# Seven products per feature added up in PSUM by two accumulating banks, and for two more features in each feed-forward block

## The chip, the cores and the metric

The kernel runs on one core of a Trainium2 chip. The metric is the device time of one execution in microseconds (us); three runs of the kernel before took 2045.32 to 2047.19 us, median 2046.94.

The engines are named as in the profile: PE is TensorE (matmuls; PEld are its weight loads), DVE is VectorE, ACT is ScalarE, POOL is GpSimd, SP is SyncE, which issues the transfers.

## The reference

Two layers of a decoder over 512 tokens of 1024 features in float32. Each layer is a feed-forward block, a mixer (gated linear attention in the first layer, retention in the second) and a second feed-forward block, each with a residual and a layer norm. The change is in the four feed-forward blocks:

```
def swiglu(x, w_in, w_out):                       # x [512, 1024], D_FF = 2816
    gate, up = jnp.split(x @ w_in, 2, axis=-1)    # w_in [1024, 5632]
    return (jax.nn.silu(gate) * up) @ w_out       # w_out [2816, 1024]

h = layer_norm(DN_ALPHA * h + 0.5 * swiglu(h, ...), g, b)
```

## The kernel before, in words

**Precision.** Every float32 operand is split exactly into hi + lo, two parts of a type that PE multiplies at full pace; a product takes three matmuls (hi hi, lo hi, hi lo), written by `mm3` (L151 to L153). ACT casts the hi part (L105 for weights, L369 for sums of h), DVE subtracts for the lo part (L106, L370).

**Weights.** They stream in granules of 1 MiB in the order of use. `Stream.prepare` splits a granule into slots of 128 x 1024: five of them, and two of 128 x 512. `Stream.next` hands out a granule and prepares the next. A plain granule takes two slots. A granule for seven products takes three and a small one, since two sums of blocks of its weights are formed (L129 to L131) and split as well.

**A feed-forward block.** The 2816 hidden features are 22 features of 128 each ("feature" below means such a group). The plain form (`feature_major`) gives gate and up of one feature with 48 matmuls of 512 columns. The form of seven products (`seven_products`; Strassen's method after Winograd over halves of the tokens, of the 1024 inputs, and of gate and up) takes 7 x 12 = 84 matmuls of 256 columns. Its products read either quarters of h as they are (`hThi`, `hTlo`) or four sums of such quarters, S0 to S3 (`Shi`, `Slo`), which `operand_sums` forms once per block, after features 0 and 1 in the program: for each of two halves c the raw sums (L364, L374, L377, L379, L382), each split by L369 and L370. The raw sums live in buffers of the tags "gate" and "up", two of each; `activate` takes its own tile `sg` from the tag "gate" as well. Features 0 to 3 of a block are plain, 4 to 21 go through seven products. After a feature ACT takes silu, DVE multiplies by up (L394), and the result is split into `ahi` (L397) and `alo` (L398), the operands of the output product. The granules of the output product ("out" in the plan, tiles `po`) lie between later features.

**PSUM.** There are six banks of the pool `acc` and two of `tr`. One feature of the seven-products form takes two of each. DVE and ACT add the products up: ACT copies the first one (L343, L349), DVE does five additions (L346 to L355).

**Order.** The order of the instructions on each engine is fixed ahead of time by a planner. It takes what is ready by its own estimate of the times, what comes first in the program going first; buffers of a tag are given out in the order of the program. On the chip each engine goes through its list in that order, with semaphores between engines.

Of the kernel before, what the change touches and what calls it, by code (L numbers as in the profile page):

```python
# [17 lines left out]
P = 128  # L18
# [8 lines left out]
FAST = frozenset(f for f in range(4, NF))  # L27
# [11 lines left out]
def _ffn_plan():  # L39
    """The order of a feed-forward block's granules: ("in", f) for gate and up of  # L40
    128 features, ("out", c, i) for four units of the output product of chunk c,
    which lie between the features of the next chunk."""
    plan = []
    for c, (f0, f1) in enumerate(CHUNKS):
        n = 0
        for f in range(f0, f1):
            plan.append(("in", f))
            if c and (f - f0) % 2 == 0 and n < (CHUNKS[c - 1][1] - CHUNKS[c - 1][0]) // 2:
                plan.append(("out", c - 1, n))
                n += 1  # L50
    return plan + [("out", len(CHUNKS) - 1, i) for i in range((CHUNKS[-1][1] - CHUNKS[-1][0]) // 2)]


def _fast():
    """The granules of feed-forward weights that seven products take."""
    r, at = set(), 0
    plan = _ffn_plan()
    for mixer in (0, GH * 3 + GH, 0, RH * 6 + 2 * RH):
        at += mixer
        r |= {at + i for i, x in enumerate(plan) if x[0] == "in" and x[1] in FAST}  # L60
        at += len(plan)
    return r
# [3 lines left out]
def tile_decoder(ctx: ExitStack, tc: tile.TileContext, a: dict, out: bass.AP):  # L66
# [9 lines left out]
    # ---------------------------------------------------------------- weights  # L76
    class Stream:
        """The weights, 1 MiB at a time in the order of their use, each split
        exactly into two float32r parts."""
# [21 lines left out]
        def parts(self, slot, src, at=0):  # L101
            """src as hi + lo."""
            n = src.shape[-1]
            hi, lo = (x[:, at:at + n] for x in slot)
            nc.scalar.copy(hi, src)  # L105
            nc.vector.tensor_sub(lo, src, hi.bitcast(F32))  # L106

        def prepare(self, i):
            if i >= self.n or i in self.split:
                return  # L110
            self.load(i)
            w = self.loaded[i]
            blk = lambda slot, c: tuple(x[:, c * B:(c + 1) * B] for x in slot)  # noqa: E731
            if i not in fast:
                s = [self.place.pop((i, c))() if (i, c) in self.place else self.slot() for c in range(2)]
                for c in range(2):
                    if i:
                        self.parts(s[c], w[:, 2 * c * B:2 * (c + 1) * B])
                    else:
                        for at in ((0, B), (B, 0))[c]:  # L120
                            self.parts(s[c], w[:, 2 * c * B + at:2 * c * B + at + B], at)
                self.split[i] = [blk(x, c) for x in s for c in range(2)]
                return
            b11, b12, b22, b21 = (w[:, c * B:(c + 1) * B] for c in range(4))
            s11, sb, st, su = (self.slot(n) for n in (1, 2, 2, 2))
            self.parts(s11, b11)
            self.parts(sb, w[:, 2 * B:])
            t13, t24 = (self.sums_pool.tile([P, 2 * B], F32, tag="sums", name="sums", bufs=2) for _ in range(2))
            nc.vector.tensor_sub(t13, w[:, B:3 * B], w[:, :2 * B])  # L129
            nc.vector.tensor_sub(t24[:, :B], b22, t13[:, :B])  # L130
            nc.vector.tensor_sub(t24[:, B:], b21, t24[:, :B])  # L131
            self.parts(st, t24)
            self.parts(su, t13)
            self.split[i] = {"b11": blk(s11, 0), "b22": blk(sb, 0), "b21": blk(sb, 1), "t2": blk(st, 0),
                             "t4": blk(st, 1), "t1": blk(su, 0), "t3": blk(su, 1)}
# [12 lines left out]
    def mm3(ps, l, r, start, stop):  # L148
        """One K tile of a float32 product: (hi + lo) x (hi + lo), with the three
        passes that reach float32's precision."""  # L150
        nc.tensor.matmul(ps, l[0], r[0], start=start, stop=False)  # L151
        nc.tensor.matmul(ps, l[0], r[1], start=False, stop=False)  # L152
        nc.tensor.matmul(ps, l[1], r[0], start=False, stop=stop)  # L153
# [4 lines left out]
    # ---------------------------------------------------------------- start  # L158
# [38 lines left out]
    # ---------------------------------------------------------------- layer norm  # L197
# [8 lines left out]
    def rsqrt(tp, out_, in_, eps, n, scale=1.0):  # L206
        """(scale * (in_ + eps)) ** -0.5"""
# [4 lines left out]
    def layer_norm(tp, t, gb, last):  # L212
        """h[t] <- LN(h[t]); its transpose into hT."""
# [22 lines left out]
    # ---------------------------------------------------------------- products  # L236
    def feature_major(w, ranges, ps=None):
        """out[feature, token] of 2 tiles of 128 features."""
# [14 lines left out]
    def two_granules_ahead():  # L253
        """The first two granules after a layer norm: the first half of the tokens
        is taken first, while the norm of the second half ends."""
# [7 lines left out]
    def token_major(t, ws2, ps):  # L263
        """out[token, 512 columns] of one token tile."""
        for k in range(KD):
            mm3(ps, pick(hT[0], slice(None), k, slice(t * P, (t + 1) * P)), ws2[k // 4][k % 4], k == 0, k == KD - 1)
# [3 lines left out]
    def add_out(t, half, ps, first, tp=None):  # L270
        """h[t] <- alpha * h[t] + ps, or h[t] + ps; with tp, what the layer norm
        needs of it."""
# [10 lines left out]
    class Units:  # L283
        """Units [P, 512] of the coming granules, four in each."""
# [9 lines left out]
    def out_steps(lhs, n, first, halves=(0, 1), tp=None):  # L294
        """h[:, half] += lhs^T @ W for all tokens, one K tile after the other: the
        steps, each to be given its unit."""
# [14 lines left out]
    def out_by_tokens(lhs, n, units, halves, first, tail=None, tp=None):  # L311
        """The same, one token tile after the other."""
# [9 lines left out]
    # ---------------------------------------------------------------- feed-forward  # L322
    def seven_products(w, s, tp):
        """gate and up [feature, token] of 128 features with the seven products of
        Winograd's form of Strassen's method, over halves of the tokens, of the
        features of h and of the outputs (gate and up)."""
# [3 lines left out]
        def bank(pool, tag):  # L330
            return pool.tile([P, 2, H], F32, tag=tag, name="products")

        def product(ps, a_, b_):
            b_ = tuple(x.rearrange("p (k c) -> p k c", k=4) for x in w[b_])
            for k in range(4):
                mm3(ps, pick(b_, slice(None), k), pick(a_, slice(None), k), k == 0, k == 3)
            return ps

        gate, up, u, v = (tp.tile([P, 2, H], F32, tag=n, name=n, bufs=1 + (n in "gateup")) for n in ("gate", "up", "u", "v"))
        x, y, z, q = (bank(*b) for b in ((pacc, "acc"), (pacc, "acc"), (ptr, "tr"), (ptr, "tr")))  # L340
        # v = (p1, p1 + p6 + p7), u = (p1 + p6, p1 + p6 + p7)
        p1 = product(x[:, 0], a11, "b11")
        nc.scalar.copy(v[:, 0], p1)  # L343
        product(z[:, 0], a12, "b21")
        p6 = product(x[:, 1], s[1], "t2")
        nc.vector.tensor_add(u[:, 0], v[:, 0], p6)  # L346
        p7 = product(y[:, 0], s[2], "t3")
        nc.vector.tensor_add(u[:, 1], u[:, 0], p7)
        nc.scalar.copy(v[:, 1], u[:, 1])  # L349
        product(z[:, 1], a22, "t4")  # L350
        nc.vector.tensor_add(gate, v, z)
        p5 = product(y[:, 1], s[0], "t1")
        nc.vector.tensor_add(up, u, p5[:, None, :].broadcast_to([P, 2, H]))
        p3 = product(q[:, 0], s[3], "b22")
        nc.vector.tensor_add(up[:, 0], up[:, 0], p3)  # L355
        return [x.rearrange("p a b -> p (a b)") for x in (gate, up)]

    def operand_sums(tp):
        """The sums of blocks of h that seven_products takes, split."""
# [26 lines left out]
    def ffn(layer, which, ln, last=False, first=False):  # L386
        with tc.tile_pool(name=f"ffn{layer}{which}", bufs=2) as tp:
# [3 lines left out]
            def activate(f, gate, up):  # L391
                sg = tp.tile([P, T], F32, tag="gate", name="sg")
                nc.scalar.activation(sg, gate, AF.Silu)
# [46 lines left out]
    # ---------------------------------------------------------------- mixers  # L440
    def gated_transpose(tp, y, n, gcol, bufs=1):
        """yT[n tiles of 128 features][tokens] * g, split."""
# [13 lines left out]
    def gla(ln):  # L456
        with tc.tile_pool(name="gla", bufs=1) as tp:
# [22 lines left out]
            def gates(pg):  # L480
                """la[head] <- log sigmoid of the gates, [key feature, token]."""
# [19 lines left out]
            def decays(hd):  # L501
                """exp of the gates' sums: within chunks of 64, and within blocks of 128
                from their start and to their end."""
# [15 lines left out]
            def qk_of(ps, d):  # L519
# [4 lines left out]
                v4 = lambda x: x.rearrange("p (n two c) -> p n two c", two=2, c=CH)  # noqa: E731  # L524
# [9 lines left out]
            def vr_of(g, between):  # L534
                """The values, and 2 silu(r); `between` is called before the last tokens."""
# [209 lines left out]
def _weights(i):  # L745
    """All matrices as granules [P, G] in the order in which the kernel takes them."""
    def blocks(w):
        """[D, 256] as four blocks of [4 x 128, 128]: (0, 0), (0, 1), (1, 1), (1, 0)."""
# [47 lines left out]
def _constants():  # L796
    """Tables that depend on the shapes alone."""
# [35 lines left out]
```

## Time and profile before

| | |
|---|---|
| median of 3 runs | 2046.94 us (2045.32 to 2047.19) |
| span of the profiled execution | 2044.7 us; the page gives no time of its own for what lies around the span |
| PE busy | 2031.3 us, 99% |
| DVE busy | 1516.3 us, 74% |
| ACT busy | 796.8 us, 39% |
| matmuls | 12364 |
| moved from and to HBM | 205.00 MB, mean 100 GB/s |
| granted TensorE clock, mean | 0.998 |

[...] Matmuls overlap in PE's pipeline, so the duration of one (0.28 us for 256 columns) is longer than the distance between the starts of two; paces are read from starts, or from counts in a window. A releaser in brackets behind a row ("<-PE fm") is what ended the engine's idle time before it.

### The profile page before, as it was taken

Reading aid. Unit: us, or ns where it says so; the run is one execution under the profiler, and the core shown is the slowest. Engines: PE = TensorE matmul, PEld = TensorE weight load, DVE = VectorE, ACT = ScalarE, POOL = GpSimd, SP = SyncE. Lnnn points to the kernel's source line nnn. Section 1 sums busy time; section 2 is a strip of 40 time slices with the busy share of each in tenths; the row PEclk is TensorE's granted clock in tenths of the full one; section 3 lists DMA queues with packets and bytes.
Section 4 is the critical chain, followed back from the end, with each engine's and each line's share of the span. In section 5 each row is a group of like instructions: output and inputs, shape, how many; then the busy total and the mean of one; then the engine's idle time right before and its main releaser. Section 6 shows DMA issues by size and latency. Waiting matters only on the chain.

```text
span 2044.7 us, 29592 instructions
## 1 busy us (share of the span) xinstructions
PE 2031.3 (99%) x12364; PEld 1808.6 (88%) x12364; DVE 1516.3 (74%) x2152; ACT 796.8 (39%) x1131; POOL 37.2 (2%) x56
## 2 busy tenths in 40 slices
PE   8999999999999999999999999999999999999998
PEld 7999998888889999998999998888888889999997
DVE  7888888745588888887888888554545468888886
ACT  5443433632234344343434443333232324443441
POOL 0000000000000000000000000000000000000000
PEclk9999999999999999999999999999999999999999
DMA  6322223112222222341322223222222222322322
GB/s 213 118 104 104 104 96 132 65 65 80 103 83 104 104 103 104 104 145 42 124 103 104 104 86 142 104 69 93 78 88 78 88 75 104 117 91 102 109 99 83
DMA packets 33637, 205.00 MB, mean 100 GB/s; under 512 B 5056, under 2 KB 5184, under 8 KB 10592
## 3 DMA queue, kind: packets, MB, share of 16 engines
q1 hardware_dynamic: 33504, 203.12, 28.2%
q8 instruction: 97, 1.59, 0.3%
q14 instruction: 36, 0.29, 0.0%
HBM read 201.00 MB, written 2.10 MB: 99 GB/s over the span
## 4 chain that ended last, share of the span: by engine, by line
PE 99%; DVE 0%; DMA 0%; ACT 0%; issue 0%; DVEq 0%
PE products L151 12%; PE products L152 12%; PE products L153 12%; PE po L151 10%; PE po L152 10%; PE po L153 10%; PE fm L152 5%; PE fm L151 5%; PE fm L153 5%; PE pvr L151 2%; PE pvr L152 1%; PE pvr L153 1%; PE pgg L151 1%; PE pgg L152 1%; PE pv L153 1%; PE pgg L153 1%
## 5 line engine op out<-in xcount | busy, mean ns | idle before, releaser
L106 DVE TENSOR_TENSOR wlo<-wf,whi 128x512 fp32r<-128x512 f32 (+1 forms) x362 | 399.6, 1108 | 97.6 <-ACT whi L105 97.2
L105 ACT CAST whi<-wf 128x512 fp32r<-128x512 f32 (+1 forms) x362 | 345.8, 958 | 300.6 <-PE po L153 130.6
L151 PE MATMUL products<-Shi,whi 128*128 128x256 f32 x1152 | 325.7, 283 | 0.0
L153 PE MATMUL products<-Shi,wlo 128*128 128x256 f32 x1152 | 325.6, 283 | 0.0
L152 PE MATMUL products<-Slo,whi 128*128 128x256 f32 x1152 | 325.6, 283 | 0.0
L151 PE MATMUL po<-whi,ahi 128*128 128x512 f32 x704 | 274.8, 391 | 0.0
L152 PE MATMUL po<-wlo,ahi 128*128 128x512 f32 x704 | 274.4, 390 | 0.0
L153 PE MATMUL po<-whi,alo 128*128 128x512 f32 x704 | 274.0, 389 | 0.0
L152 PE MATMUL products<-hTlo,whi 128*128 128x256 f32 x864 | 243.0, 281 | 0.0
L151 PE MATMUL products<-hThi,whi 128*128 128x256 f32 x864 | 242.9, 281 | 0.0
L153 PE MATMUL products<-hThi,wlo 128*128 128x256 f32 x864 | 242.0, 280 | 0.0
L153 PEld LDWEIGHTS products<-Shi,wlo 128*128 128x128 f32 x1152 | 220.4, 191 | 0.0
L151 PEld LDWEIGHTS products<-Shi,whi 128*128 128x128 f32 x1152 | 220.0, 191 | 0.3
L152 PEld LDWEIGHTS products<-Slo,whi 128*128 128x128 f32 x1152 | 220.2, 191 | 0.0
L105 ACT CAST whi<-sums 128x1024 fp32r<-128x1024 f32 x144 | 150.3, 1047 | 159.8 <-DVE h L277 87.7
L151 PE MATMUL fm<-hThi,whi 128*128 128x512 f32 (+1 forms) x592 | 202.9, 343 | 5.2 <-ACT hThi L183 5.2
L152 PE MATMUL fm<-hTlo,whi 128*128 128x512 f32 (+1 forms) x592 | 203.0, 343 | 0.0
L153 PE MATMUL fm<-hThi,wlo 128*128 128x512 f32 (+1 forms) x592 | 202.5, 342 | 0.0
L106 DVE TENSOR_TENSOR wlo<-sums,whi 128x1024 fp32r<-128x1024 f32 x144 | 175.7, 1222 | 24.0 <-ACT whi L105 24.0
L152 PEld LDWEIGHTS products<-hTlo,whi 128*128 128x128 f32 x864 | 163.0, 189 | 1.4
L151 PEld LDWEIGHTS products<-hThi,whi 128*128 128x128 f32 x864 | 162.9, 189 | 1.4
L153 PEld LDWEIGHTS products<-hThi,wlo 128*128 128x128 f32 x864 | 163.5, 189 | 0.0
(185 smaller groups left out, 3431.0 us busy)
## 6 DMA issues: line engine op xcount, KB each, us to landing
wf<-in_wts SPq DMA_DIRECT2D x179, 1024.0 KB, 4.8
ln_b<-in_ln_b SPq DMA_DIRECT2D x6, 512.0 KB, 3.7
ln_g<-in_ln_g SPq DMA_DIRECT2D x6, 512.0 KB, 5.2
xs<-in_xT SPq DMA_DIRECT2D x8, 256.0 KB, 5.3
h<-in_x SPq DMA_DIRECT2D x4, 512.0 KB, 7.8
out_h<-h SPq DMA_DIRECT2D x8, 256.0 KB, 2.0
wf<-in_wts SPq DMA_DIRECT2D x4, 256.0 KB, 5.8
dm<-in_decay SPq DMA_DIRECT2D x4, 256.0 KB, 3.2
```

Source lines behind the costliest of these rows:

```text
L105: nc.scalar.copy(hi, src)
L106: nc.vector.tensor_sub(lo, src, hi.bitcast(F32))
L151: nc.tensor.matmul(ps, l[0], r[0], start=start, stop=False)
L152: nc.tensor.matmul(ps, l[0], r[1], start=False, stop=False)
L153: nc.tensor.matmul(ps, l[1], r[0], start=False, stop=stop)
```

## The change

Features 2 and 3 of each block go through seven products too (`FAST` begins at 2). Inside `seven_products`, four products are added into one PSUM bank x one after the other, two into a bank z, and one goes to a bank y. After each step but the last the running sum is copied out of the bank by ACT into a tile `part` before the next product adds to it; DVE's five additions become three of 256 columns. The second half of gate is left in x, and `activate` reads it from there. The bank tiles are half as large, but each still takes a bank (two of `acc`, one of `tr` per feature). `operand_sums`, the plan, the numbers of slots and the tags "gate" and "up" stay. A parameter lowers the scratch for DMAs that are generated on the fly.

```diff
-FAST = frozenset(f for f in range(4, NF))
+FAST = frozenset(f for f in range(2, NF))
...
-    def mm3(ps, l, r, start, stop):
+    def mm3(ps, l, r, start, stop, more=False):
...
+        nc.tensor.matmul(ps, l[0], r[0], start=start, stop=False, skip_group_check=more)
...
         def bank(pool, tag):
-            return pool.tile([P, 2, H], F32, tag=tag, name="products")
+            return pool.tile([P, H], F32, tag=tag, name="products")
...
+        def product(ps, a_, b_, start=True):
...
+                mm3(ps, pick(b_, slice(None), k), pick(a_, slice(None), k), start and k == 0, k == 3, not start)
+
+        def kept(ps, n):
+            nc.scalar.copy(part[:, n], ps)
+            return part[:, n]
+
+        part = tp.tile([P, 4, H], F32, tag="part", name="part", bufs=2)
+        gate, up = (tp.tile([P, 2, H], F32, tag=n, name=n) for n in ("gate", "up"))
+        x, y, z = (bank(*b) for b in ((pacc, "acc"), (ptr, "tr"), (pacc, "acc")))
+
+        product(x, a11, "b11")
+        p1 = kept(x, 0)
+        product(y, a12, "b21")
+        nc.vector.tensor_add(gate[:, 0], p1, y)
+        product(x, s[1], "t2", False)
+        p16 = kept(x, 1)
+        product(z, s[0], "t1")
+        p5 = kept(z, 3)
+        product(x, s[2], "t3", False)
+        p167 = kept(x, 2)
+        product(z, s[3], "b22", False)
+        nc.vector.tensor_add(up[:, 1], p167, p5)
+        nc.vector.tensor_add(up[:, 0], p16, z)
+        product(x, a22, "t4", False)
+        return gate, up, x
...
-            def activate(f, gate, up):
+            def activate(f, gate, up, late=None):
                 sg = tp.tile([P, T], F32, tag="gate", name="sg")
-                nc.scalar.activation(sg, gate, AF.Silu)
+                if late is None:
+                    nc.scalar.activation(sg, gate, AF.Silu)
+                else:
+                    nc.scalar.activation(sg[:, :H], gate[:, 0], AF.Silu)
+                    nc.scalar.activation(sg[:, H:], late, AF.Silu)
+                    up = up.rearrange("p a b -> p (a b)")
...
-    nc = bacc.Bacc("TRN2", target_bir_lowering=False, num_devices=1)
+    nc = bacc.Bacc("TRN2", target_bir_lowering=False, num_devices=1, dynamic_dma_scratch_size=1024)
```

## Rows read from the trace of the kernel before

**Rows 1.** The page's parts 1 and 4: engines' busy time, shares of the chain.

```profile
PE 2031.3 (99%) x12364; PEld 1808.6 (88%) x12364; DVE 1516.3 (74%) x2152; ACT 796.8 (39%) x1131; POOL 37.2 (2%) x56
...
PE 99%; DVE 0%; DMA 0%; ACT 0%; issue 0%; DVEq 0%
```

**Rows 2.** Waits of PE: who for whom, us in total, times, longest.

```profile
PE fm L151 <- ACT hThi L183: 5.2, 1, 5.2
PE po L151 <- ACT yhi L450: 0.3, 1, 0.3
```

**Rows 3.** Windows: stretch, length, busy us per engine, granted clock, DMA.

```profile
core 0: us, PE busy (x) PEld busy (x) DVE busy (x) ACT busy (x) POOL busy (x), PEclk, DMA share, GB/s
602.11:624.51 22.40, 22.40 (x98) 18.05 (x97) 21.89 (x32) 11.41 (x18) 0.00 (x0) 1.00 0.27 93
645.42:665.43 20.01, 20.01 (x169) 20.00 (x168) 15.55 (x22) 10.16 (x15) 0.00 (x0) 1.00 0.22 80
376.00:379.40 3.40, 3.40 (x8) 2.71 (x9) 2.07 (x3) 3.38 (x8) 0.00 (x0) 0.51 0.40 169
```

**Rows 4.** Timeline of DVE, second block: start, duration, engine, line, operation, tiles, shapes.

```profile
589.66 1.30 DVE L364 TENSOR_TENSOR hsum<-hThi,hTlo 128x512 f32<-128x512 f32 x2
596.70 0.69 DVE L394 SCALAR_TENSOR_TENSOR sg<-sg,fm 128x512 f32<-128x512 f32 x1 [5.74 <-PE fm L153]
...
600.18 0.69 DVE L364 TENSOR_TENSOR hsum<-hThi,hTlo 128x512 f32<-128x512 f32 x1
...
604.86 0.69 DVE L398 TENSOR_TENSOR alo<-sg,ahi 128x512 fp32r<-128x512 f32 x1
...
606.59 0.68 DVE L364 TENSOR_TENSOR hsum<-hThi,hTlo 128x512 f32<-128x512 f32 x1
607.19 1.22 DVE L106 TENSOR_TENSOR wlo<-wf,whi 128x1024 fp32r<-128x1024 f32 x1
608.33 0.68 DVE L377 TENSOR_TENSOR hsum<-hsum 128x512 f32<-128x512 f32 x1
608.93 0.69 DVE L130 TENSOR_TENSOR sums<-wf,sums 128x512 f32<-128x512 f32 x1
...
618.57 0.69 DVE L370 TENSOR_TENSOR Slo<-hsum,Shi 128x512 fp32r<-128x512 f32 x1
```

**Rows 5.** Timelines of PE and DVE: starts of feature 2, ends of S1.

```profile
30.31 0.40 PE L151 MATMUL fm<-hThi,whi 128*128 128x512 f32 x1
602.11 0.40 PE L151 MATMUL fm<-hThi,whi 128*128 128x512 f32 x1
951.71 0.40 PE L151 MATMUL fm<-hThi,whi 128*128 128x512 f32 x1
...
46.20 0.69 DVE L370 TENSOR_TENSOR Slo<-hsum,Shi 128x512 fp32r<-128x512 f32 x1
968.17 0.69 DVE L370 TENSOR_TENSOR Slo<-hsum,Shi 128x512 fp32r<-128x512 f32 x1
```

**Rows 6.** Timeline of PE in the first block's feature 4.

```profile
55.54 0.40 PE L151 MATMUL products<-Shi,whi 128*128 128x256 f32 x2
```

**Rows 7.** Timeline of PE ahead of the slow stretch.

```profile
372.29 3.69 PE L487 MATMUL pz<-gl,wgate 32*128 32x512 f32 x8
```

**Rows 8.** Timelines of PE and ACT at the end of a product.

```profile
652.32 0.28 PE L152 MATMUL products<-hTlo,whi 128*128 128x256 f32 x1
...
652.69 1.05 ACT L105 CAST whi<-sums 128x1024 fp32r<-128x1024 f32 x1 [0.49 <-PE products L152]
653.65 0.62 ACT L393 ACTIVATE sg<-gate 128x512 f32<-128x512 f32 x1
```

**Rows 9.** Groups by line: busy us, mean ns, idle before and releaser.

```profile
L129 DVE TENSOR_TENSOR sums<-wf 128x1024 f32<-128x1024 f32 x72 | 87.9, 1221 | 1.0
L351 DVE TENSOR_TENSOR gate<-v,products 128x512 f32<-128x512 f32 x72 | 49.5, 688 | 70.4 <-PE products L153 68.5 <-ACT v L349 1.9
L343 ACT COPY v<-products 128x256 f32<-128x256 f32 x72 | 26.9, 373 | 37.3 <-PE products L153 37.0
```

More of the change, by code (lines that the diff above doesn't have):

```diff
@@ L146, in tile_decoder @@
     ws = Stream()
-    def mm3(ps, l, r, start, stop):
-        nc.tensor.matmul(ps, l[0], r[0], start=start, stop=False)
-        nc.tensor.matmul(ps, l[0], r[1], start=False, stop=False)
-        nc.tensor.matmul(ps, l[1], r[0], start=False, stop=stop)
+    def mm3(ps, l, r, start, stop, more=False):
+        nc.tensor.matmul(ps, l[0], r[0], start=start, stop=False, skip_group_check=more)
+        nc.tensor.matmul(ps, l[0], r[1], start=False, stop=False, skip_group_check=more)
+        nc.tensor.matmul(ps, l[1], r[0], start=False, stop=stop, skip_group_check=more)
     def pick(pair, *idx):
@@ L330, in bank @@
         def bank(pool, tag):
-            return pool.tile([P, 2, H], F32, tag=tag, name="products")
-        def product(ps, a_, b_):
+            return pool.tile([P, H], F32, tag=tag, name="products")
+        def product(ps, a_, b_, start=True):
             b_ = tuple(x.rearrange("p (k c) -> p k c", k=4) for x in w[b_])
             for k in range(4):
-                mm3(ps, pick(b_, slice(None), k), pick(a_, slice(None), k), k == 0, k == 3)
-            return ps
-        gate, up, u, v = (tp.tile([P, 2, H], F32, tag=n, name=n, bufs=1 + (n in "gateup")) for n in ("gate", "up", "u", "v"))
@@ L340, in seven_products @@
[L340 to L356, printed above, removed]
+                mm3(ps, pick(b_, slice(None), k), pick(a_, slice(None), k), start and k == 0, k == 3, not start)
+        def kept(ps, n):
+            nc.scalar.copy(part[:, n], ps)
+            return part[:, n]
```

## The prediction

> **What bounds the kernel now.** Read the page's first and fourth parts before anything else [rows 1]: TensorE (PE) is busy for 99% of the span and the chain of work that ended last is 99% PE. Then the list of waits, for PE alone [rows 2]: two waits in the whole run, 5.2 us at the start and 0.3 us. So the time is the number of matmuls times their pace, and any wait that the change puts on PE is paid in full. The table of windows gives the paces [rows 3]. From 602.11 to 624.51 PE does features 2 and 3 of the second feed-forward block in the plain form, 96 matmuls of 512 columns (2 x 48; the count includes those on the edges): 22.40/96 = 0.2333 us. From 645.42 to 665.43 it does two features with seven products, 168 matmuls of 256 columns: 20.01/168 = 0.1191 us. The same rows carry the warning: VectorE (DVE) is busy for 21.89 of the 22.40 us under features 2 and 3, against 15.55 of 20.01 later. Something is being made ready there.
>
> The timeline of DVE over that place says what [rows 4]: the sums of blocks of h (L364 to L382, their splits at L370) that every seven-products feature needs. Feature 2 starts at 602.11; the split of S1's second half, needed by a feature's third product, starts at 618.57 and ends 0.69 later, at 619.26, 17.1 us after the start of feature 2. In the first block it ends at 46.20 + 0.69, 16.6 us after feature 2's start at 30.31; in the third at 968.17 + 0.69, 17.1 us after 951.71 [rows 5]. Before the change nothing minds: features 2 and 3 are plain, and cover 22.4 us.
>
> **The change, part by part.** I sum on the profiled execution: 2044.7 us of span, and the 2.2 us by which the median of the runs shown (2046.94) exceeds it I take as lying around the span and unchanged.
>
> (a) Two more features in each of four blocks go through seven products. Removed: 48 x 0.2333 = 11.20 us each; added: 84 x 0.1191 = 10.00. Eight times 1.20: **-9.6 us**. That is the whole gain, since PE does the same seven products per feature otherwise.
>
> (b) The sums lose their cover. Call feature 2's start t. Its first two products read h itself and take 24 x 0.119 = 2.86 us; the third reads S1, so S1's second half is wanted at t + 2.86 + 0.71 = t + 3.6. It cannot be there: the chain stands in a queue for buffers. The raw sums share two buffers of tag "gate" with the two activations before them. In the trace, after two sums of the other tag (589.66), DVE does nothing for 5.74 us before 596.70 although h is complete; the first "gate" sum runs at 600.18, and the second at 606.59, behind alo of feature 1 at 604.86 [rows 4]. The edit leaves tags, counts and order alone. From the second "gate" sum to the end of S1's second half it is 619.26 - 606.59 = 12.67 us, of which L106 at 607.19 (1.14 to the next start) and L130 at 608.93 (0.60) are foreign; without them 10.9. Lower bound: alo's 0.60 from 604.86, then 10.9: 616.4 or t + 14.3. Upper bound: features 2 and 3 now want the seven-products split of their weights too. On DVE one such split is 1.14 for L129 (1.22 busy [rows 9], but a 1024-wide row lets the next start after 1.14, as at 607.19), twice 0.60, 0.60 for b11 and 3 x 1.14 = 6.4 us, against 2 x 1.14 = 2.3 plain; the 4.1 more for feature 2, if none of it falls into the idle stretch, puts it at t + 21.2. I take the row itself, t + 17.1: the extra split fits the idle 5.74 us, and the foreign work inside the chain is only exchanged.
>
> What can PE do in those 17.1 us? Feature 2's first two products (2.86), the first halves of its third and of the one on S0 (1.42, their sums come first), the two products of feature 3 that read h (2.86), and one of feature 4 (1.43): 8.6. The order on each engine is a planner's by readiness, not the program's: at 55.54, in the first block, two L151 matmuls on S start one behind the other [rows 6], where the program writes each L151 with its L152 and L153 behind it: one of the two was drawn forward from a later product. So PE idles about 8.5 us in each block, with 5.0 at the lower bound (t + 14.3, and 9.3 filled by half a product more) and 17.6 at the upper one (t + 21.2, and nothing filled but 3.6). Four blocks: **+34 us**, bounds +20 and +70.
>
> (c) The clock. After 372.29, where PE had eight small matmuls in 3.69 us [rows 7], the granted clock is 0.51 for 3.4 us (376.00 to 379.40 [rows 3]): 1.7 us lost. PE's idle stretch here is at least as empty. One such loss in each block: **+6.8 us**, none to two per block as bounds (0 to +13.6).
>
> (d) The accumulating banks. The second product into a bank waits until ScalarE has copied the first; a product into another bank lies between (1.43 us). A copy costs 0.37 [rows 9], so alone it is hidden. But three products on, the last split of the next weights becomes free to start: in [rows 8] such a cast starts at 652.69, 0.37 us after the start of the last-but-one matmul of the product that frees its buffer (652.32), and ScalarE's next instruction starts 0.96 later. The new copy of p1+p6+p7 would stand behind that cast: it would end 0.37 + 0.96 + 0.37 = 1.70 after that matmul, and the accumulating product is due 0.24 + 1.43 = 1.67 after it. Late by 0.03, and with an exposed answer and weight load perhaps 0.25 for each of 80 features: 0 to +20. I take the 0.03: **+2 us**.
>
> [...]
>
> (e) At nothing: fewer DVE additions (three of 256 columns and two of 512, each of the latter 0.69 [rows 9], become three of 256) and more ScalarE copies (two become four, and silu is halved) work on engines with room in the steady stretch, DVE 15.55 and ScalarE 10.16 busy in 20.01 us [rows 3]; PE's cover there is the 10 us of each feature. They would cost only through (d). The single banks, the smaller scratch of the DMA and the dropped comments issue nothing.
>
> Sum: -9.6 + 34 + 6.8 + 2 = +33; 2044.7 + 2.2 + 33 = **2080 us**.
>
> **The rivals.**
>
> *Faster: the sums arrive in time.* If the raw sums ran in DVE's idle 5.74 us, or enough foreign products filled PE, only (a) would remain: 2046.9 - 9.6 = 2037. For it: DVE is free there. Against it: the decisive second "gate" sum comes behind alo of feature 1, which itself starts 2.75 us after t (604.86 against 602.11), and the edit moves neither. It decides from S1 ready at t + 3.6. Chance 0.09. If the idle time is just eaten by the gain, 2.4 us per block, the time stays within 0.2% (4 us, about what a measurement of this kernel tells from no change): 2047, chance 0.06.
>
> *Slower still: nothing fills the wait.* PE then idles 17.1 - 3.6 = 13.5 us a block, with two clock losses: -9.6 + 54 + 13.6 + 2 = +60, 2107 us. For it: a blocked matmul blocks those behind it if the order was planned on other times than the chip's. Against it: [rows 6]. Chance 0.14. [...]
>
> *Slower by the copies.* If every feature pays 0.25 us in (d), 18 us come on top: 2098. For it: the cast becomes ready one matmul before the copy. Against it: the planner can put a matmul of the next feature into so short a gap. Chance 0.10.
>
> **How the numbers follow.** The forecast has 0.55, in a range of its own of 2057 (the lower bound of (b), no clock loss, no late copies) to 2105; 0.06 more I leave to slower mixtures of these. Slower by over 0.2%: 0.55 + 0.14 + 0.10 + 0.06 = 0.85; within 0.06; faster 0.09. The range takes in the forecast, the late copies and half of the unfilled case: 2050 to 2112.
>
> **What would show it.** In PE's waits, four long ones on DVE's Slo at products of features 2, near 33, 605 and 955 us and in the fourth block, 5 to 14 us each block; a granted clock of half after them; PE's products at 0.119 us elsewhere. The split of S1's second half still 14 to 21 us after the start of feature 2. For (d), many short waits of products on a ScalarE copy, once a feature. The prediction is wrong if PE's list of waits stays as short as before, if S1 is ready within 4 us of feature 2's start, or if PE's waits in the blocks sum to less than 10 us.

## The result, and the profile after

The changed kernel takes 2083.38 us (median of 4 runs, 2082.48 to 2084.57), the kernel before 2046.81 us beside it: a ratio of 1.0178, 95% interval 1.0164 to 1.0193. It is slower by 36.6 us, 37 in round figures. The profiled execution has a span of 2082.6 us, against 2044.7 before.

From the page of after, its parts 1 and 4, against [rows 1]:

```profile
PE 2048.1 (98%) x12652; PEld 1831.4 (88%) x12652; DVE 1459.4 (70%) x2072; ACT 875.9 (42%) x1403; POOL 37.2 (2%) x56
...
PE 96%; DVE 3%; ACT 0%; issue 0%; DMA 0%; DVEq 0%; SPq 0%; ACTq 0%
```

DVE is in the chain now, with 3% of the span. The list of PE's waits in after (who for whom, us in total, times, longest), against [rows 2], says where:

```profile
PE products L151 <- ACT Shi L374: 14.0, 8, 2.7
PE fm L151 <- ACT hThi L183: 5.4, 1, 5.4
PE products L152 <- DVE Slo L375: 5.3, 8, 0.9
PE products L151 <- ACT part L340: 1.1, 4, 0.3
PE po L151 <- ACT yhi L460: 0.3, 1, 0.3
```

Sixteen waits on the sums of h, four in each block, and four on a copied partial sum: 14.0 + 5.3 + 1.1 = 20.4 us, 5.1 a block. The waits on hThi (the start) and on yhi are there as before. In the second block of after the timeline of PE has feature 2's start, the four waits on sums, and the one on a copy:

```profile
611.56 0.28 PE L151 MATMUL products<-hThi,whi 128*128 128x256 f32 x1
...
619.32 0.50 PE L151 MATMUL products<-Shi,whi 128*128 128x256 f32 x2 [0.90 <-ACT Shi L374]
620.47 0.39 PE L152 MATMUL products<-Slo,whi 128*128 128x256 f32 x1 [0.65 <-DVE Slo L375]
...
624.13 0.58 PE L151 MATMUL products<-Shi,whi 128*128 128x256 f32 x1 [2.68 <-ACT Shi L374]
625.29 0.58 PE L152 MATMUL products<-Slo,whi 128*128 128x256 f32 x1 [0.57 <-DVE Slo L375]
...
630.37 0.58 PE L151 MATMUL products<-Shi,whi 128*128 128x256 f32 x1 [0.25 <-ACT part L340]
```

and the timeline of DVE there has alo of feature 1, the second raw sum of tag "gate" behind it, and the splits of S1's first half, S0's second half and S1's second half, against [rows 4]:

```profile
614.32 0.68 DVE L408 TENSOR_TENSOR alo<-sg,ahi 128x512 fp32r<-128x512 f32 x1
...
615.52 0.69 DVE L369 TENSOR_TENSOR hsum<-hThi,hTlo 128x512 f32<-128x512 f32 x1
...
619.74 0.68 DVE L375 TENSOR_TENSOR Slo<-hsum,Shi 128x512 fp32r<-128x512 f32 x1
...
624.55 0.68 DVE L375 TENSOR_TENSOR Slo<-hsum,Shi 128x512 fp32r<-128x512 f32 x1
...
626.96 0.68 DVE L375 TENSOR_TENSOR Slo<-hsum,Shi 128x512 fp32r<-128x512 f32 x1
```

With feature 2's start as t, the second raw sum is at t + 4.0 and S1 is complete at 627.64, t + 16.1; in the other three blocks at t + 16.2, 15.6 and 16.1. (`operand_sums` splits S0, S2, S1 and S3 of the first half c, then those of the second; in a block's eight splits the third is S1's first half, the fifth S0's second and the seventh S1's second.) The first pair of waits ends with S1's first half, at 619.74 + 0.68; the second pair, with the longest wait, ends with S0's second half, at 624.55 + 0.68 or t + 13.7. S1's second half, though later, ends no wait in the list: PE is then at work, at a granted clock of 0.50 (windows below).

The four windows of after in which the granted clock (the share of its full speed at which PE was allowed to run) is half (stretch, length, then busy us of PE, PEld, DVE, ACT and POOL, clock, DMA) begin within the third and longest wait of their block, in the third block 0.17 us after it (983.27):

```profile
41.36:48.19 6.83, 4.50 (x16) 3.80 (x17) 6.83 (x11) 2.79 (x5) 0.00 (x0) 0.50 0.00 0
621.63:631.87 10.24, 6.86 (x26) 5.86 (x27) 9.54 (x15) 3.48 (x7) 0.00 (x0) 0.50 0.00 0
983.44:990.27 6.83, 5.82 (x22) 4.85 (x23) 6.83 (x11) 2.86 (x6) 0.00 (x0) 0.50 0.00 0
1754.85:1761.68 6.83, 5.35 (x19) 4.36 (x19) 6.83 (x11) 3.14 (x7) 0.00 (x0) 0.50 0.00 0
```

In these 30.7 us PE is busy for 22.5 us with 83 matmuls; at 0.1191 each they would take 9.9. At half clock the starts are 0.21 us apart instead of 0.12 (eight steps from 628.00 to 629.71 in PE's timeline), and 0.38 behind a wait (630.37 to 630.75). So half clock, with the slow starts in it, costs 12.6 us beside the waits.

There is a third loss that no list of waits shows. In the steady stretch of after one matmul of each feature is late. ACT at such a place, then PE, then PEld:

```profile
88.05 1.05 ACT L105 CAST whi<-sums 128x1024 fp32r<-128x1024 f32 x1 [0.95 <-PE products L152]
89.00 0.37 ACT L340 COPY part<-products 128x256 f32<-128x256 f32 x1
```

```profile
89.29 0.28 PE L153 MATMUL products<-Shi,wlo 128*128 128x256 f32 x1
89.42 0.39 PE L151 MATMUL products<-hThi,whi 128*128 128x256 f32 x1
89.65 0.28 PE L152 MATMUL products<-hTlo,whi 128*128 128x256 f32 x1
```

```profile
89.17 0.19 PEld L153 LDWEIGHTS products<-Shi,wlo 128*128 128x128 f32 x1
89.42 0.19 PEld L151 LDWEIGHTS products<-hThi,whi 128*128 128x128 f32 x1
```

The copy of p1 + p6 + p7 stands behind a cast and ends at 89.37; the seventh product adds to the same bank and starts at 89.42. Its weight load starts with it instead of 0.12 after the load before it, so 0.23 us pass to the next start instead of 0.12. Over the trace such a place is 0.104 us over the pace.

### The profile page after: what moved, and what is told of

It is laid out like the page before. It is cut to its first block, busy times and chain, and to the rows that moved or that the text cites. A ratio compares the mean times of both kernels' runs of the same rounds, so it can differ in the third digit from the quotient of the medians.

```text
span 2082.6 us, 30225 instructions
## 1 busy us (share of the span) xinstructions
PE 2048.1 (98%) x12652; PEld 1831.4 (88%) x12652; DVE 1459.4 (70%) x2072; ACT 875.9 (42%) x1403; POOL 37.2 (2%) x56
## 4 chain that ended last, share of the span: by engine, by line
PE 96%; DVE 3%; ACT 0%; issue 0%; DMA 0%; DVEq 0%; SPq 0%; ACTq 0%
PE products L151 13%; PE products L152 13%; PE products L153 13%; PE po L151 10%; PE po L152 10%; PE po L153 10%; PE fm L151 3%; PE fm L152 3%; PE fm L153 3%; PE pvr L151 1%; PE pvr L153 1%; PE pvr L152 1%; PE pgg L151 1%; PE pv L153 1%; PE pgg L152 1%; PE pv L151 1%
## 5 line engine op out<-in xcount | busy, mean ns | idle before, releaser
L151 PE MATMUL products<-Shi,whi 128*128 128x256 f32 x1280 | 368.3, 288 | 15.5 <-ACT Shi L374 14.0
L152 PE MATMUL products<-Slo,whi 128*128 128x256 f32 x1280 | 366.4, 286 | 5.3 <-DVE Slo L375 5.3
L153 PE MATMUL products<-Shi,wlo 128*128 128x256 f32 x1280 | 364.4, 285 | 0.0
L151 PE MATMUL products<-hThi,whi 128*128 128x256 f32 x960 | 276.6, 289 | 0.0
L151 PE MATMUL po<-whi,ahi 128*128 128x512 f32 x704 | 274.7, 390 | 0.0
L152 PE MATMUL po<-wlo,ahi 128*128 128x512 f32 x704 | 274.6, 390 | 0.0
L153 PE MATMUL po<-whi,alo 128*128 128x512 f32 x704 | 274.3, 390 | 0.0
L153 PE MATMUL products<-hThi,wlo 128*128 128x256 f32 x960 | 269.4, 281 | 0.0
L152 PE MATMUL products<-hTlo,whi 128*128 128x256 f32 x960 | 269.4, 281 | 0.0
L151 PEld LDWEIGHTS products<-Shi,whi 128*128 128x128 f32 x1280 | 248.7, 195 | 20.2 <-ACT Shi L374 15.6
L152 PEld LDWEIGHTS products<-Slo,whi 128*128 128x128 f32 x1280 | 248.8, 194 | 7.5 <-DVE Slo L375 7.5
L153 PEld LDWEIGHTS products<-Shi,wlo 128*128 128x128 f32 x1280 | 248.8, 195 | 0.0
L151 PEld LDWEIGHTS products<-hThi,whi 128*128 128x128 f32 x960 | 180.5, 188 | 6.1 <-ACT part L340 0.7
L152 PEld LDWEIGHTS products<-hTlo,whi 128*128 128x128 f32 x960 | 180.8, 188 | 1.3
L153 PEld LDWEIGHTS products<-hThi,wlo 128*128 128x128 f32 x960 | 180.6, 188 | 0.0
L340 ACT COPY part<-products 128x256 f32<-128x256 f32 x320 | 118.8, 371 | 128.8 <-PE products L153 128.4
L277 DVE TENSOR_TENSOR h<-h,po 128x512 f32<-128x512 f32 x168 | 113.9, 684 | 63.1 <-PE po L153 63.0
L151 PE MATMUL fm<-hThi,whi 128*128 128x256 f32 (+1 forms) x464 | 152.2, 328 | 5.4 <-ACT hThi L183 5.4
```

The lines of the kernel that those rows point to most:

```text
L151: nc.tensor.matmul(ps, l[0], r[0], start=start, stop=False, skip_group_check=more)
L152: nc.tensor.matmul(ps, l[0], r[1], start=False, stop=False, skip_group_check=more)
L153: nc.tensor.matmul(ps, l[1], r[0], start=False, stop=stop, skip_group_check=more)
L277: nc.vector.tensor_add(x, x, ps)
L340: nc.scalar.copy(part[:, n], ps)
```

## The experiments

Each kernel was timed beside the kernel before (2046.0 to 2047.3 us in these comparisons), and its time is the median of 5 to 11 runs.

**acc_from4: the accumulating banks alone.**

```diff
-FAST = frozenset(f for f in range(2, NF))
+FAST = frozenset(f for f in range(4, NF))
```

> The accumulating banks alone: features 2 and 3 plain again (FAST from 4), everything else as after. My theory: the trace of after shows in each feature of the steady stretch one matmul of 0.39 us with 0.22 us to the next start, 0.104 us over the pace, where the seventh product follows the copy of p1+p6+p7 (a copy at 89.00 behind a cast at 88.05). With 72 such features: 72 x 0.104 = 7.5 us over before, 2054 us; no wait of PE on a Shi or Slo; granted clock of half only where before has it. Rival 1 (the prediction's own figure, 0.03 us each): 2049. Rival 2 (0.25 us each): 2065. Rival 3 (the banks cost nothing, all 37 us are the two more features): 2047.

2054.51 us, ratio 1.0033 (1.0021 to 1.0046). PE waits nowhere in the blocks, the clock falls only at the mixer and at the end as before (0.998 in the mean in both), and 72 matmuls are late, 7.6 us together by the distances between starts. The theory holds to half a microsecond; the prediction's 0.03 us and the rival's 0.25 us for each feature are both wrong.

**acc4_dve_reads_x: is it the copy?**

```diff
-        p167 = kept(x, 2)
-        product(z, s[3], "b22", False)
-        nc.vector.tensor_add(up[:, 1], p167, p5)
+        nc.vector.tensor_add(up[:, 1], x, p5)
+        product(z, s[3], "b22", False)
```

> acc_from4 without the copy of p1+p6+p7: DVE adds p5 to it straight from bank x, so the seventh product waits for DVE and not for the copy behind ScalarE's cast; ScalarE has 72 copies fewer, DVE as many additions as before. My theory (the 7.2 us of acc_from4 are this one copy behind a cast, 0.104 us in each of 72 features; DVE is idle there): 2047 us, and the 72 late matmuls are gone from the trace. Rival 1 (adding on in a bank has a price of its own, whoever reads it): 2054. Rival 2 (DVE's weight subtraction of 1.22 us takes the cast's place): late matmuls remain, 2050 to 2060.

2045.75 us, ratio 0.9999 (0.9990 to 1.0007): the 7 us are gone. DVE, idle there, adds at 90.94, as soon as p7 is in the bank, and PE keeps its pace into the seventh product (timelines of DVE and PE of this kernel):

```profile
90.94 0.42 DVE L356 TENSOR_TENSOR up<-products,part 128x256 f32<-128x256 f32 x1 [2.56 <-PE products L153]
```

```profile
91.98 0.28 PE L153 MATMUL products<-Shi,wlo 128*128 128x256 f32 x1
92.11 0.28 PE L151 MATMUL products<-hThi,whi 128*128 128x256 f32 x1
92.22 0.28 PE L152 MATMUL products<-hTlo,whi 128*128 128x256 f32 x1
```

So adding on in a bank costs nothing that the interval (2 us either way) would show: the other three copies of a feature stay and PE's pace stays with them (0.11 to 0.13 us between the starts above). The one copy that stood behind a cast was the whole price.

**old_from2: the two more features alone.** The diff is the one line `FAST` of the change, in the kernel before.

> The two more features alone: the old seven_products with its five DVE additions, FAST from 2. My theory: the loss of after less the 80 x 0.104 = 8.3 us of the copies, so 2075 us; eight waits of PE on Shi and eight on Slo, some 20 us together, and half the granted clock for 25 to 31 us in the four blocks. Rival 1 (the new wait is caused by ScalarE's extra copies, since PE waits for ScalarE's Shi): the waits shrink to under 10 us together and the time is below 2060. Rival 2 (DVE's five additions make the sums later still): over 2083.

2081.51 us, ratio 1.0160 (1.0146 to 1.0174): slower by 34 us, where the theory said 28. Its waits of PE:

```profile
PE products L151 <- ACT Shi L369: 13.5, 5, 2.8
PE products L151 <- issue: 7.1, 3, 2.5
...
PE products L151 <- ACT whi L105: 3.1, 4, 0.8
PE products L152 <- DVE Slo L370: 2.7, 5, 0.8
```

That is 26.4 us, and 37.5 us at half clock in the blocks, though S1 is complete at the same t + 16.1 (15.6 to 16.1) as in after. (This execution is the slowest of the five, 2084.20 us. It also waits 1.7 us for hThi at 11.76 and has 3.4 us at half clock from there, which after has not.) Both rivals fall by their mechanism: ScalarE's extra copies don't cause the waits, and the sums aren't later. The theory's 2075 us fell too. The traces show where the old form waits longer for the same sums: in each block PE does 36 matmuls of seven products before its first wait, in after 54. Why its order has fewer to offer was not tried. The two parts of the change, 7 and 34 us, come to 41 where the whole is 37.

**no_sums: no sums to wait for.** The four products on S0 to S3 read quarters of h; the sums are left out.

```diff
-            s = operand_sums(tp)
+            s = [pick(hT[0], slice(None), ks, ts) for ks in (LOW, HIGH) for ts in HALVES]
```

> After without the sums of h: the four products that read S0 to S3 read quarters of h instead, so the sums, their casts and their subtractions are left out; the same matmuls otherwise. My theory: nothing waits, the clock stays, the gain of (a) of 9.4 us remains, and the copies cost 80 x 0.104 = 8.3: 2046 us. Rival 1 (the waits come from ScalarE and DVE being behind with the larger weight split of features 2 and 3, not from the sums): waits of PE on whi or wlo take their place and the time stays over 2060. Rival 2 (the copies cost nothing): 2037.

2043.74 us, ratio 0.9982 (0.9973 to 0.9991). The window over feature 2 of the second block and what follows has PE busy throughout, at full clock:

```profile
600.00:620.00 20.00, 19.98 (x166) 19.55 (x165) 14.70 (x20) 11.40 (x22) 0.00 (x0) 1.00 0.31 107
```

So about 40 of the changed kernel's 2083 us hang on the sums, and without them the larger weight split of features 2 and 3 keeps PE from nothing. (DVE and ScalarE have less to do as well without the sums; that PE waited for the sums themselves is what its list of waits in after says.) That the time comes 2 us under the theory has the sign of matmuls that read h following each other a little faster (0.1183 against 0.1199 us in after, last section); this was not tried by itself.

**sums_in_part and own_raw: other buffers for the raw sums.** The first puts them into the buffers of `part`, the second into two of a tag of their own:

```diff
+            raw = tp.tile([P, 4, H], F32, tag="part", name="raw", bufs=2)   # own_raw: tag="raw"
...
-                x = tp.tile([P, 2, H], F32, tag=tag, name="hsum")
+                x = raw[:, tag:tag + 2] if tag in (0, 2) else tp.tile([P, 2, H], F32, tag=tag, name="hsum")
...
-            x21 = full(0, HALVES[1], "gate")
+            x21 = full(0, HALVES[1], 0)
...
-            x11 = full(0, HALVES[0], "gate")
+            x11 = full(0, HALVES[0], 2)
```

> After with the two raw sums of each half c that had buffers of tag gate put into one of the two buffers of tag part (whose first other user is the copy of p1 of feature 2 or 3), so that they no longer stand in line with sg of features 0 and 1. My theory (the buffers make the sums late, DVE has idle time ahead of them): S1's second half is ready at least 6 us sooner, the waits of PE on Shi and Slo fall from 19 us to under 5, the half clock goes with them, and the time is 2045 to 2058. Rival 1 (DVE's work itself is the limit: the sums take the time that the chain of copy and subtraction takes, wherever they lie): the waits keep over 12 us and the time is over 2072.

> After with the raw sums of tag gate in two buffers of their own and nothing else: order of the sums and the copies as in after. My theory (the buffers alone make most of the lateness; what sums_in_part kept was partly the copy of p1 behind a raw sum): waits of PE on Shi and Slo under 4 us, 2050 to 2059 us, of which 8 are the late copies. Rival 1 (DVE's work is the limit): as sums_in_part or later, 2060 or more.

2060.66 us (ratio 1.0063, 1.0051 to 1.0076) and 2060.08 us (1.0062, 1.0050 to 1.0075): 23 us of the 37 come back by nothing but a buffer, and the order that the planner makes with it. In own_raw S1 is complete at t + 9.0 in the first block instead of t + 16.2 (5.4 to 10.3 in the others), and half clock is left in 3.4 us of the blocks instead of 30.7. Feature 2's start and the split of S1's second half there (timelines of PE and DVE):

```profile
30.70 0.28 PE L151 MATMUL products<-hThi,whi 128*128 128x256 f32 x1
...
39.06 0.68 DVE L377 TENSOR_TENSOR Slo<-raw,Shi 128x512 fp32r<-128x512 f32 x1
```

The waits left in sums_in_part:

```profile
PE products L152 <- DVE Slo L377: 1.9, 3, 0.8
PE products L151 <- ACT whi L105: 1.7, 5, 0.4
PE products L151 <- ACT Shi L376: 1.5, 3, 0.6
PE products L151 <- ACT part L340: 0.7, 2, 0.3
PE products L153 <- DVE wlo L106: 0.7, 2, 0.3
```

The theory's waits on sums under 5 us came (1.9 + 1.5), its time for sums_in_part did not: 2.4 us of waits on weight parts are new, and the next start of PE behind a wait comes after 0.22 us instead of 0.12 (612.50 to 612.72 in its timeline). own_raw's 2060 is just over the theory and the very number of its rival, that DVE's work is the limit; sharing `part` made no difference. Both hold in part: the buffers made most of the lateness (waits on sums 3.6 us, S1 seven us sooner), and some is left that is not theirs.

**filler: is the half clock a consequence of idling?**

```diff
+        if f == 2:
+            for _ in range(3):
+                product(bank(ptr, "tr"), a12, "b21")
         product(x, s[1], "t2", False)
```

> After with 36 more matmuls of 256 columns (three further copies of the second product, their result unused) in feature 2 of each block, ahead of the third product: 4.3 us of work where PE idles 5.1 us a block. My theory (the half clock is what the idle stretch leaves behind, and costs some 15 us of the 36): idle time falls from 20 to about 4 us, the half clock of 31 us in the four blocks goes, and the time falls to 2064 to 2072 although PE does 144 matmuls more. Rival 1 (the clock falls for another reason, such as the products themselves): the half clock stays, 2080 to 2086. Rival 2 (the filler takes the place of products drawn forward, so the wait stays as long): 2090 to 2100.

2080.50 us, ratio 1.0168 (1.0154 to 1.0181). Waits, and two windows, the first at the place of after's longest slow stretch:

```profile
PE products L152 <- DVE Slo L378: 3.1, 4, 0.8
PE products L151 <- ACT Shi L377: 2.9, 7, 0.5
...
PE products L151 <- ACT part L340: 1.3, 4, 0.3
```

```profile
621.63:631.87 10.24, 8.32 (x60) 7.13 (x58) 9.71 (x16) 5.35 (x11) 0.00 (x0) 1.00 0.01 2
1754.54:1757.95 3.41, 3.16 (x15) 2.82 (x14) 3.41 (x6) 1.02 (x3) 0.00 (x0) 0.50 0.02 5
```

The idle time falls from 20.4 to 7.3 us, and the half clock from 30.7 to 3.4 us (one block): with PE kept at work, the clock stays. The time came 8.5 us over the forecast, within the numbers of rival 1, whose half clock did not stay. 144 matmuls cost 144 x 0.119 = 17.1; the idle time that they fill is no gain, and I had counted it as one. By the rows: +17.1 for the filler, -13.1 of waits, -12.6 + 1.7 of half clock is -6.9; the span fell by 4.7.

**s1_first_dve and own_raw_s1_first: a version that waits for nothing?** Raw sums in other buffers (`part` in the first, own ones in the second), S0 and S1 of both halves before S2 and S3, and DVE's reading of x as above:

```diff
+        for c in range(2):
...
+            parts(c, s1, 0)
...
+            parts(c, x11, 1)
+            raw.append((x21, x11))
+        for c, (x21, x11) in enumerate(raw):
+            parts(c, x21, 2)
+            x12 = full(c, 4, HALVES[0])
+            nc.vector.tensor_sub(x12, x12, x11)
+            parts(c, x12, 3)
```

> After with three edits: the raw sums in the buffers of tag part (as in sums_in_part), S0 and S1 of both halves of h formed before S2 and S3 (as DVE's work ahead of S1's second half was the limit there), and bank x read by DVE in place of the copy of p1+p6+p7. My theory: S1 is ready within 7 us of feature 2's start, PE has no wait on a sum over 0.5 us, no half clock in the blocks, and the gain of (a) remains: 2047 - 9.4 + up to 3 = 2038 to 2041 us, below before and after. Rival 1 (ScalarE's casts for S2 and S3 or for the weights become the bound): waits on Shi or whi keep 10 us or more, 2048 to 2060. Rival 2 (the copy wasn't the cost of the banks): 2045 to 2048.

> s1_first_dve with the raw sums in two buffers of a tag of their own instead of the buffers of part (part is a quarter smaller, since the copy of p1+p6+p7 is gone): the copy of p1 then waits for no sum, which was the 7.8 us of waits on part in s1_first_dve. My theory: no wait of PE over 0.5 us in the blocks but the first start, no half clock beside the one of the mixer, 2047 - 9.4 + up to 4 = 2037 to 2042 us. Rival 1 (the wait moves to the next in line, S2 or S3 or the weights' hi parts): 5 us of waits or more remain and the time is over 2044.

2051.67 us (ratio 1.0027, 1.0016 to 1.0037) and 2050.15 us (1.0015, 1.0006 to 1.0024); both miss. In the first PE waits for the copy of p1, whose `part` buffer still holds a raw sum:

```profile
PE products L151 <- ACT part L340: 7.8, 3, 3.3
```

In the second that wait is gone and smaller ones, 5.2 us in all, stand in its place. Its third block, from first matmul to first matmul of the next stage, takes 347.3 us against before's 349.6, the full 2.3 of (a); the other three still lose 2.0 to 2.5 us on before. Two windows of the second block show why:

```profile
585.00:605.00 20.00, 20.00 (x172) 19.97 (x171) 20.00 (x32) 9.80 (x14) 0.92 (x1) 1.00 0.30 106
605.00:620.00 15.00, 13.36 (x101) 12.12 (x100) 15.00 (x25) 7.05 (x13) 0.00 (x0) 1.00 0.05 12
```

The third busy figure is DVE's: 35.00 of 35.00 us. With the buffers out of the way, DVE's own work is the bound here; the last run of this section gives DVE more time and bears it out.

**old_from2_sums_early: without the banks.** `old_from2` with the same order and buffers of the raw sums (and the smaller DMA scratch, for room).

> The old seven_products with five DVE additions, FAST from 2, with the raw sums in buffers of their own and S0 and S1 first (and the smaller DMA scratch of after, for room): no accumulating banks. My theory (the gain is in the two features alone, and the sums' lateness was the whole loss of old_from2): the waits of 26 us fall under 4, and the time is 2037 to 2043. Rival 1 (without the accumulating banks DVE has too much to do for the sums, since old_from2 waited longer than after): waits of 6 us or more, 2046 to 2060.

2056.38 us, ratio 1.0045 (1.0032 to 1.0057): 25 us better than old_from2, 6 worse than own_raw_s1_first. The rival's numbers came. The waits have moved to DVE's additions and to weights:

```profile
PE products L151 <- DVE u L348: 4.6, 3, 1.5
PE po L151 <- ACT whi L105: 3.0, 4, 0.8
PE products L152 <- DVE Slo L370: 2.2, 5, 0.7
```

So with the old form, too, early sums alone don't bring the time under before; that DVE's additions are the reason is what the waits on `u` suggest, not more.

**from3 and from3_sums_early: a plain feature 2 as cover.** `FAST` from 3, in after and in own_raw_s1_first.

> After with FAST from 3: feature 2 is plain again and covers 11.2 us, feature 3 goes through seven products. My theory (the loss is the lateness of S1, ready 16 us after feature 2's start; feature 3 wants it 11.2 + 3.6 = 14.8 us after that, and PE can fill several us): no wait of PE on a sum over 0.5 us, no half clock in the blocks, 2054.5 - 4 x 1.17 + 4 x 0.104 = 2050 us. Rival 1 (each added feature costs its half, so half of the 29 us between acc_from4 and after): 2069. Rival 2 (the larger weight splits of fast features ahead of the sums make S1 later by the time that feature 2 covers): over 2060.

> own_raw_s1_first with FAST from 3: the same early sums and DVE's reading of x, but feature 2 of each block plain. In own_raw_s1_first DVE is busy for 35.00 of the 35.00 us from 585 to 620, so DVE's own work had become the bound there; a plain feature 2 gives it 11.2 us more and a weight split less. My theory: no wait of PE on a sum, a weight part or a sum of products in the blocks, no half clock in them, and half of (a): 2047 - 4 x 1.17 = 2042 us (2040 to 2044), under before. Rival 1 (DVE's work stays the bound, the plain feature moves it only): waits of 4 us or more, 2045 to 2050.

from3: 2052.56 us, ratio 1.0032 (1.0019 to 1.0044); no wait on a sum, no half clock in the blocks, 2.5 us over the theory. from3_sums_early: 2042.43 us, ratio 0.9980 (0.9971 to 0.9989), as forecast, 4 us under before and 41 under after. Whether it needs the accumulating banks was not tried: no run has the old form with early sums and `FAST` from 3. Its whole list of PE's waits, with nothing left in the feed-forward blocks but the first start:

```profile
PE fm L151 <- ACT hThi L183: 5.2, 1, 5.2
PE pgo L603 <- DVE st L594: 0.4, 1, 0.4
PE po L151 <- ACT yhi L464: 0.3, 1, 0.3
```

## Why the prediction was right, point by point

The time (2080 forecast, 2083.4 measured) and the mechanism, the sums' lost cover, were right. Three of the five terms were not, and they offset one another, so that the time came out within 4 us is in part luck.

| term | predicted | after against before |
|---|---|---|
| (a) two more features | -9.6 | -9.4: plain matmuls 321.4 to 231.9 us, 672 products at 0.1192 are +80.1 |
| (b) waits for the sums | +34 (20 to 70) | +20.4, by the waits |
| (c) half clock | +6.8 (0 to 13.6) | +12.6, by the windows |
| (d) late copies | +2 (0 to 20) | +8.3: 80 x 0.104 |
| (e) fewer additions, more copies | 0 | 0 beside (d): acc4_dve_reads_x |
| starts after a wait, outside the half clock | none | +2.1, by the distances between starts |

These make +34; the span grew by 37.9. An estimate places 2 of the missing 4 us just ahead of the waits: a wait is counted from the end of the matmul before it, 0.28 us after that one's start, where the next would have started after 0.12, and twelve of the twenty waits begin outside the half clock, 12 x 0.16 = 1.9. The other 2 are not assigned.

(a) [rows 3] gave the two paces, and both held.

(b) S1's lateness was read well: t + 16.1 against t + 17.1 from [rows 4, 5], with the second "gate" sum at t + 4.0, behind alo of feature 1. That the buffers are most of the reason is shown by own_raw, and that the sums are the whole loss of the two features by no_sums. But S1's second half is not what PE waits for last, as the sum in (b) has it. The planner draws S0's product ahead of S1's, and the last wait on a sum ends with S0's second half, at t + 13.7. Even the filling was right: until S1 is complete PE does 71 matmuls in the second block, 71 x 0.119 = 8.5 us of work against the 8.6 counted. What was mis-sized is the price: 16.1 - 8.5 = 7.6 us are lost up to there, of which the list has only 4.8 as waits. The rest is slow starts and work at half pace, which I had as idle time in (b) and again, too small, in (c). Taken together (b) and (c) were forecast at 41 us and came to 37: 20.4 + 12.6 + 2.1 + 1.9. The forecast of four long waits, near t + 3, failed in form: PE fills first, then waits four times a block at t + 7 to t + 14, at most 2.7 us each.

(c) One slow stretch of 3.4 us a block was taken from the mixer [rows 3, 7]. The blocks have 6.8 to 10.2 us each, and the loss is close to the upper bound. filler shows that idling is the cause: with the idle time down from 20.4 to 7.3 us, the half clock is down from 30.7 to 3.4.

(d) The rows were right [rows 8]: the copy stands behind the cast, in nearly every feature, and the seventh product starts about 0.01 us late (in the 72 places of acc_from4 0.131 after the matmul before it, not 0.12). The price of that was not: the matmul behind it comes another 0.104 us late. The rows show the product's weight load late with it. The upper bound's 0.25, with "an exposed answer" in it, stands in no row and was an estimate of mine; of the two that it names the late load is what the rows show, and the place costs 0.104.

The rivals: the sums in time (2037) and the idle time just eaten by the gain (2047) fall by S1 at t + 16.1; no kernel here reached 2037. Nothing filling the wait (2107) falls by the 71 matmuls. What was said for it, that a blocked matmul blocks those behind it, the second block of after shows: the L153 at 625.67 reads the same part of `Shi` as the L151 at 624.13, and starts 0.38 us behind the L152 that waited 0.57 us for `Slo`. Copies at 0.25 us each (2098) falls by acc_from4.

## What to carry to other kernels

When an edit takes cover from a chain, cost the wait, the slow clock after it (0.50 for 30.7 us here) and the work done at that clock together; the list of waits shows only a part (20.4 of 37 us here). Look for what the waiting engine draws forward, since another link of the chain may then end the wait. The buffers that hold the chain up are the cheapest thing to change (23 of 37 us here). When the running sum of a PSUM bank must be read before the next product, look at what stands ahead of the reader in its queue, and let the engine that is idle there read it (7 us here). A stretch that looks free because one engine waits for buffers may be full as soon as they are there: DVE, idle for 5.74 us in one stretch before, was busy for 35 of 35 us.

## What the runs showed of the hardware

A late matmul need not leave a gap: acc_from4 lost 7.2 us with no idle time of PE beside before's; only a duration of 0.39 for 0.28 us tells of it, and in after a weight load that starts with its matmul (89.42) instead of 0.12 us ahead (89.17 for 89.29).

Over the whole trace of after, outside waits and half clock, PE's products on S follow each other at 0.1199 us (3641 steps) and those on h at 0.1183 (2681), with the same shapes; in the kernel before it is 0.1197 and 0.1182. For 48 matmuls on S in each of 80 features that makes 6 us. What makes the difference was not tried.
